# Low halves of split weights: adding transfers that read DRAM instead of the raw tile, sums of weights in place, six raw tiles

## The chip, the cores and the metric

The kernel runs on one core of one Trainium2 chip. The metric is device time in microseconds of the whole program, one launch. Times of several runs are given by their median. The page and the trace come from one further execution that was profiled.

## What is computed

Two layers of a trunk act on 640 tokens (128 context, 512 latent) of width 1024. Each layer has a half-step feed-forward, a mixer (windowed attention, pooling, short convolution) and a second half-step feed-forward; shift, scale and gate of each come from a modulation by `w_ada`. Cut to the part that matters here:

```
def ffn_sublayer(x, mod, k, g, w_in, w_out):
    h = modulated_norm(x, mod, k, g)
    gt, up = jnp.split(h @ w_in, 2, axis=-1)          # w_in: 1024 x 5632
    return x + 0.5 * mod[:, None, 3 * k + 2] * ((jax.nn.silu(gt) * up) @ w_out)   # w_out: 2816 x 1024

def trunk_layer(x, mod, ...):
    x = ffn_sublayer(x, mod, 0, norm_g[0], w_ffn_in[0], w_ffn_out[0])
    h = modulated_norm(x, mod, 1, norm_g[1])
    q, k, v, u_pool, u_conv, bg, cg = jnp.split(h @ w_in, IN_SPLITS, axis=-1)
    ...
    y = jnp.concatenate([attn, pool, conv], axis=-1) @ w_out
    x = x + mod[:, None, 5] * y
    return ffn_sublayer(x, mod, 2, norm_g[2], w_ffn_in[1], w_ffn_out[1]), k, v
```

All tensors are float32.

## The kernel before

Tokens lie along the free dimension, in two halves of 320 columns; channels lie on the 128 partitions. TensorE (PE) multiplies in float32r, a reduced form of float32. To keep float32's precision each operand is split in two: a high half `h` or `wh`, which is the operand rounded to float32r, and a low half `wl`, the rest. `mm3` (L351 to L354) then makes three products onto one accumulator: high by high (L352), high by low (L353), low by high (L354).

How a weight gets its halves is the matter here. A load on the SP queue brings 128 columns of a weight (or 256 of an output weight) into a raw tile of 128 x 1024 (`raw_tile`, L142; pool `raw`, five tiles). `split_w` (L164) has ScalarE (ACT) copy it to `wh` (L170), which rounds, and copy `-wh` to `wl` (L173). Then GpSimd (POOL) issues a DMA whose source is the raw tile and which adds to what stands in `wl` (L174): `wl = raw - wh`. The transfer runs on the 16 DMA engines that also run the loads. POOL's instruction at L174 is the issue alone. With another engine given, `split_w` subtracts there instead (L176). There are four `wh` and four `wl` tiles of full size and two small ones.

Weights are prefetched as far as tiles allow: the Tile scheduler orders each engine's instructions ahead of time and decides which tile takes over which buffer; a load on the SP queue waits until the buffer's last reader is done, and the loads behind it in the queue wait with it.

The feed-forward (`ffn`, L556) goes over 22 columns of 128 hidden channels (index `j`), each with an upper weight and a gate weight, and after every four or five of them multiplies the finished ones with rows of the output weight (`down`, L618; `update_x`, L518, adds the result to the residual on DVE). In the first feed-forward all columns are plain (`up`, L602). In the other three the first three are plain and 19 are fast (`fast_ups`, L690): seven products of half size instead of eight, by sums of weights. `fast_weights` (L640) loads the upper weight (halves a1, a2) and the gate weight (d1, d2), and DVE makes four sums (L646) into two tiles of a pool `sums` (`sum_tile`, L145; two tiles):

```
one = [a1+d1, d1+d2]      two = [d1+d2+a1, d1+d2+a1+a2]
products use: 1 = a1, 2 = a2, 4 = d2, 3 = two's second half, 6 = two's first, 5 = one's second, 7 = one's first
```

The upper weight and d2 get their low half from an adding transfer (512 KB and 256 KB), the two tiles of sums by subtraction on DVE (L176). On PE the order in a column is 1, then 3 and 4 of the column before, then 6, 2, 7, 5.

The modulation (`ada_steps`, L293) runs beside the feed-forwards: each step loads a 512 KB piece of `w_ada` into a raw tile. In the first feed-forward DVE sums over it into a tile of `sums` (L309, L311); later PE multiplies it directly (L275). `sums` also gives the tile that takes transposed probabilities in the attention (L1116). The last feed-forward carries no modulation.

The first column's weights are handled apart (`first_tiles`, L1218): `weights(0, nc.gpsimd)` splits the first pair by adding transfers, `weights(1, nc.vector)` the second by DVE.

## Time and profile before

| | us |
|---|---|
| median of three runs (2467.55 to 2479.46) | 2470.77 |
| profiled execution | 2474.73 |
| its span, first to last instruction | 2472.9 |
| PE busy | 2341.6 (95%) |
| PE weight loads busy | 2250.0 (91%) |
| DVE busy | 1324.6 (54%) |
| ACT busy | 1217.4 (49%) |
| POOL busy | 317.4 (13%) |

The stages lie at about these places of the span: first feed-forward to 490 us, mixer to 760, second feed-forward to 1240, then the second layer's feed-forward to 1700, mixer to 2010 and last feed-forward to the end. PE's weight loads run beside its products. DMA-issuing instructions of SP are not counted as busy; POOL's issue of a transfer is. "DMA share" is the mean busy share of the 16 DMA engines. Queue q1 is that of the loads issued by SP, q0 that of the transfers issued by POOL. A row of the timeline gives the start, the duration, the instruction, and in brackets how long its engine was idle before it and what ended that.

### The profile page before, as it was taken

To read this page: it belongs to the slowest core of one execution; us is meant where nothing else is said; L and a number is where in the kernel's file an instruction comes from. 1 tells how busy PE (TensorE), PEld (TensorE's weight loads), DVE (VectorE), ACT (ScalarE), POOL (GpSimd) and SP (SyncE) were. 2 spreads that over 40 slices of the span, in tenths; PEclk is the share of its full clock that TensorE was granted. 3 is DMA by queue.
4 is the path that set the end of the run, shared out by engine and by line. 5 is a ranking of instruction groups with operands and counts; after the bars stand their busy time and mean duration, and the time that the engine had idled before them with its cause. 6 is when DMAs were issued, how large, how long until landed. Compare 5 with 4: busy or idle time off the path is not lost.

```text
span 2472.9 us, 41585 instructions
## 1 busy us (share of the span) xinstructions
PE 2341.6 (95%) x16594; PEld 2250.0 (91%) x16594; DVE 1324.6 (54%) x2907; ACT 1217.4 (49%) x2080; POOL 317.4 (13%) x383
## 2 busy tenths in 40 slices
PE   7899999999999999989999999899999999999999
PEld 6899999989978998979999989899898789999999
DVE  4546565455868444345465353454557675445453
ACT  4433333445668444344565353445456675455461
POOL 1111111111100111110101111111111001111110
PEclk9999999999999999999999999999999999999999
DMA  8869798766524776775866767767665236666563
GB/s 279 208 160 247 184 258 196 206 144 137 134 56 116 191 161 180 166 196 141 204 144 157 159 146 170 176 151 174 153 129 130 59 81 132 155 130 162 131 156 101
DMA packets 388826, 393.13 MB, mean 159 GB/s; under 512 B 31032, under 2 KB 306840, under 8 KB 388632
## 3 DMA queue, kind: packets, MB, share of 16 engines
q1 hardware_dynamic: 340932, 244.88, 32.9%
q0 software_dynamic: 47520, 145.51, 32.7%
q8 instruction: 131, 2.15, 0.4%
q14 instruction: 63, 0.52, 0.1%
q10 hardware_dynamic: 180, 0.07, 0.0%
HBM read 242.04 MB, written 2.88 MB: 99 GB/s over the span
## 4 chain that ended last, share of the span: by engine, by line
PE 55%; issue 19%; DMA 16%; DVE 5%; ACT 3%; POOL 1%; POOLq 0%; ACTq 0%; SPq 0%; DVEq 0%
PE acc L352 16%; PE acc L353 16%; PE acc L354 16%; DMA wl<-raw 7%; DMA raw<-in_w_ffn_in 7%; POOL wl L174 1%; PE mis L275 1%; DMA raw<-in_w_ada 1%; DVE sums L646 1%; ACT wl L173 1%; PE acc L1060 1%; PE po L352 1%; PE mis L1111 1%; PE po L353 1%; PE po L354 1%
## 5 line engine op out<-in xcount | busy, mean ns | idle before, releaser
L352 PE MATMUL acc<-h,wh 128*128 128x320 f32 (+1 forms) x2808 | 886.4, 318 | 59.1 <-ACT part L671 24.5
L354 PE MATMUL acc<-h,wl 128*128 128x320 f32 (+1 forms) x2808 | 875.9, 313 | 15.5 <-DMA wl<-raw 15.4
L353 PE MATMUL acc<-h,wh 128*128 128x320 f32 (+1 forms) x2808 | 878.6, 314 | 0.6 <-DVE h L156 0.6
L170 ACT ACTIVATE wh<-raw 128x1024 fp32r<-128x1024 f32 (+2 forms) x332 | 305.5, 921 | 662.4 <-PE acc L353 438.1
L352 PEld LDWEIGHTS acc<-h,wh 128*128 128x128 f32 x2808 | 535.2, 191 | 81.3 <-ACT part L671 29.9
L354 PEld LDWEIGHTS acc<-h,wl 128*128 128x128 f32 x2808 | 535.8, 191 | 20.4 <-DMA wl<-raw 20.2
L174 POOL DMA_DIRECT2D wl<-raw x330 | 287.7, 872 | 2049.3 <-ACT wl L173 1425.5
L353 PEld LDWEIGHTS acc<-h,wh 128*128 128x128 f32 x2808 | 536.5, 191 | 2.9 <-POOL h L412 0.8
L352 PE MATMUL acc<-g,wh 128*128 128x320 f32 x1408 | 444.1, 315 | 33.5 <-DVE x L518 33.5
L353 PE MATMUL acc<-g,wh 128*128 128x320 f32 x1408 | 442.1, 314 | 0.0
L354 PE MATMUL acc<-g,wl 128*128 128x320 f32 x1408 | 441.3, 313 | 0.0
L518 DVE SCALAR_TENSOR_TENSOR x<-acc,gate,x 128x128 f32<-128x128 f32 (+2 forms) x480 | 195.3, 436 | 285.1 <-PE acc L354 283.8
L173 ACT ACTIVATE wl<-wh 128x1024 fp32r<-128x1024 f32 (+2 forms) x330 | 302.6, 917 | 4.7
L352 PEld LDWEIGHTS acc<-g,wh 128*128 128x128 f32 x1408 | 270.4, 192 | 37.9 <-DVE x L518 26.3
L353 PEld LDWEIGHTS acc<-g,wh 128*128 128x128 f32 x1408 | 270.6, 192 | 0.3
L354 PEld LDWEIGHTS acc<-g,wl 128*128 128x128 f32 x1408 | 270.2, 192 | 0.7 <-DMA wl<-raw 0.5
L170 ACT ACTIVATE wh<-sums 128x1024 fp32r<-128x1024 f32 x114 | 120.6, 1057 | 163.6 <-PE acc L353 145.9
L176 DVE TENSOR_TENSOR wl<-sums,wh 128x1024 fp32r<-128x1024 f32 x114 | 139.6, 1225 | 66.4 <-ACT wh L170 64.9
L646 DVE TENSOR_TENSOR sums<-raw 128x512 f32<-128x512 f32 x114 | 74.7, 688 | 167.5 <-DMA raw<-in_w_ffn_in 167.0
L311 DVE SCALAR_TENSOR_TENSOR sums<-raw,c,sums 128x512 f32<-128x512 f32 x196 | 134.7, 744 | 38.3 <-DMA raw<-in_w_ada 38.3
L671 ACT ACTIVATE part<-acc 128x320 f32<-128x320 f32 x171 | 72.9, 426 | 42.5 <-PE acc L354 42.4
L156 DVE TENSOR_TENSOR g<-part,g 128x320 fp32r<-128x320 f32 x114 | 56.0, 492 | 68.5 <-ACT g L155 67.6
(200 smaller groups left out, 2470.4 us busy)
## 6 DMA issues: line engine op xcount, KB each, us to landing
wl<-raw POOLq DMA_DIRECT2D x209, 512.0 KB, 5.2
raw<-in_w_ffn_in SPq DMA_DIRECT2D x176, 512.0 KB, 5.0
raw<-in_w_ada SPq DMA_DIRECT2D x128, 512.0 KB, 5.2
raw<-in_w_ffn_out SPq DMA_DIRECT2D x48, 512.0 KB, 4.2
raw<-in_w_ffn_out SPq DMA_DIRECT2D x64, 320.0 KB, 4.2
wl<-raw POOLq DMA_DIRECT2D x64, 320.0 KB, 4.5
wl<-raw POOLq DMA_DIRECT2D x57, 256.0 KB, 4.7
raw<-in_w_in SPq DMA_DIRECT2D x20, 512.0 KB, 5.7
```

Source lines behind the costliest of these rows:

```text
L156: nc.vector.tensor_tensor(lo, src, f32(h), op=ALU.subtract)
L170: nc.scalar.activation(h, raw, AF.Copy)
L173: nc.scalar.activation(lo, f32(h), AF.Copy, scale=-1.0)
L174: eng.dma_start(lo, raw, accum_op=ALU.add)
L176: eng.tensor_tensor(lo, raw, f32(h), op=ALU.subtract)
L311: nc.vector.scalar_tensor_tensor(part[:, j, :], r[:, k, :], c, part[:, j, :], op0=ALU.mult, op1=ALU.add)
L352: nc.tensor.matmul(out, wh, xh, start=start, stop=False, skip_group_check=onto)
L353: nc.tensor.matmul(out, wh, xl, start=False, stop=False, skip_group_check=onto)
L354: return nc.tensor.matmul(out, wl, xh, start=False, stop=stop, skip_group_check=onto)
L518: nc.vector.scalar_tensor_tensor(xT[t][:, s:e], ps[:, s - a : e - a], gates[l][n][:, t, j : j + 1], xT[t][:, s:e], op0=ALU.mult, op1=ALU.add,)
L646: add = lambda out, x, y: nc.vector.tensor_tensor(out, x, y, op=ALU.add)
L671: nc.scalar.activation(t, ps[:, :HALF], AF.Copy)
```

## The change

Four edits. The adding transfer reads the weight's columns from DRAM once more, by the same access pattern as the load, instead of the raw tile (`adding`; every load function now takes the function that starts the transfer). The sums of weights are made in place in the two raw tiles: afterwards the gate tile holds d1+d2 and a1+d1+d2, the upper tile a1+d1 and the sum of all four; both are then split by DVE as before. Pool `sums` goes; the raw pool has six tiles in place of five, and also gives the modulation's accumulator in the first feed-forward and the attention's tile. The first pair of weights is subtracted on POOL instead of by adding transfers. The scratch for descriptors that POOL writes grows from 1024 to 4096.

```
-    rawp = pool("raw", 5)
+    rawp = pool("raw", RAW)
-    sump = pool("sums", 2)
...
         raw = (raw or raw_tile())[:, : nk * width].rearrange("p (k c) -> p k c", k=nk)
-        loads(raw)
-        return raw, nk, width
+        loads(raw, nc.sync.dma_start)
+        return raw, nk, width, loads
+    def adding(dst, src):
+        nc.gpsimd.dma_start(dst, src, accum_op=ALU.add)
...
-    def split_w(raw, nk, width, eng=nc.gpsimd):
+    def split_w(raw, nk, width, loads=None, eng=None):
...
         nc.scalar.activation(h, raw, AF.Copy)
-        if eng is nc.gpsimd:
+        if eng is None:
             nc.scalar.activation(lo, f32(h), AF.Copy, scale=-1.0)
-            eng.dma_start(lo, raw, accum_op=ALU.add)
+            loads(lo, adding)
         else:
             eng.tensor_tensor(lo, raw, f32(h), op=ALU.subtract)
...
-            lambda raw: nc.sync.dma_start(raw, src[:, c0 : c0 + width].rearrange("(k p) c -> p k c", p=P)),
+            lambda dst, start: start(dst, src[:, c0 : c0 + width].rearrange("(k p) c -> p k c", p=P)),
...
-            part = sum_tile().rearrange("p (j c) -> p j c", j=2)
+            part = raw_tile().rearrange("p (j c) -> p j c", j=2)
...
-            one, two = view(sum_tile()), view(sum_tile())
-            ups = split_w(up, KD, P)
-            add(one[:, :nk, :], a1, d1)
-            add(one[:, nk:, :], d1, d2)
-            add(two[:, :nk, :], one[:, nk:, :], a1)
-            add(two[:, nk:, :], two[:, :nk, :], a2)
-            late = split_w(d2, nk, P)
-            twos = split_w(two, KD, P, nc.vector)
-            ones = split_w(one, KD, P, nc.vector)
+            ups = split_w(up, KD, P, up_loads)
+            late = split_w(d2, nk, P, lambda dst, start: start(
+                dst, w_in[D // 2 :, j * P : (j + 1) * P].rearrange("(k p) c -> p k c", p=P)))
+            add(a1, a1, d1)
+            add(d1, d1, d2)
+            add(d2, a1, d2)
+            add(a2, d2, a2)
+            gates = split_w(gate, KD, P, eng=nc.vector)
+            both = split_w(up, KD, P, eng=nc.vector)
...
-                    pts = sum_tile("pts")[:, :512]
+                    pts = raw_tile()[:, :512]
...
-            ws.extend(split_w(*raws[2 * j + s], eng=eng) for s in range(2))
+            ws.extend(split_w(*raws[2 * j + s][:3], eng=eng) for s in range(2))
...
-    nc = bacc.Bacc("TRN2", target_bir_lowering=False, num_devices=1, dynamic_dma_scratch_size=1024)
+    nc = bacc.Bacc("TRN2", target_bir_lowering=False, num_devices=1, dynamic_dma_scratch_size=4096)
```

Two places of the order are shown. First POOL's queue of adding transfers in the last fast columns of the second layer's first feed-forward; a row names destination, source, and partitions x elements (before) or partitions x pieces x elements (now). Before:

```order
L174 DMA wl<-raw 128x1024
L174 DMA wl<-raw 128x512
L174 DMA wl<-raw 128x1024
L174 DMA wl<-raw 128x512
L174 DMA wl<-raw 128x1024
L174 DMA wl<-raw 128x512
```

Now, the last columns and the output weights behind them:

```order
L162 DMA wl<-in_w_ffn_in 128x8x128
L162 DMA wl<-in_w_ffn_in 128x4x128
L162 DMA wl<-in_w_ffn_in 128x8x128
L162 DMA wl<-in_w_ffn_in 128x4x128
L162 DMA wl<-in_w_ffn_in 128x8x128
L162 DMA wl<-in_w_ffn_in 128x4x128
L162 DMA wl<-in_w_ffn_out 128x4x256 x8
```

The sequence of large and small transfers is as it was; the source is DRAM, and each partition's share is eight or four pieces of 128 elements.

Second the sums on DVE in the last feed-forward, one fast column and the start of the next (`part` are partial products, `g` the gated result). Before:

```order
L683 TENSOR_TENSOR part<-acc,part 128x320
L156 TENSOR_TENSOR g<-part,g 128x320
L675 TENSOR_TENSOR part<-acc,part 128x320
L687 TENSOR_TENSOR part<-part 128x320
L156 TENSOR_TENSOR g<-part,g 128x320
L675 TENSOR_TENSOR part<-po,part 128x320
L176 TENSOR_TENSOR wl<-sums,wh 128x1024
L646 TENSOR_TENSOR sums<-raw 128x512 x2
L176 TENSOR_TENSOR wl<-sums,wh 128x1024
L675 TENSOR_TENSOR part<-acc,part 128x320
L646 TENSOR_TENSOR sums<-sums,raw 128x512 x2
```

Now:

```order
L683 TENSOR_TENSOR part<-acc,part 128x320
L646 TENSOR_TENSOR raw<-raw 128x512
L153 TENSOR_TENSOR g<-part,g 128x320
L675 TENSOR_TENSOR part<-acc,part 128x320
L646 TENSOR_TENSOR raw<-raw 128x512 x2
L687 TENSOR_TENSOR part<-part 128x320
L646 TENSOR_TENSOR raw<-raw 128x512
L153 TENSOR_TENSOR g<-part,g 128x320
L675 TENSOR_TENSOR part<-po,part 128x320
L176 TENSOR_TENSOR wl<-raw,wh 128x1024 x2
L675 TENSOR_TENSOR part<-acc,part 128x320
```

The four sums stood around the two subtractions and belonged to the column after; now they stand ahead of the two subtractions that read them, between the column's other work.

## Rows read from the trace of the kernel before

**Rows 1.** The page: busy us (share of the span) xinstructions, by engine

```profile
PE 2341.6 (95%) x16594; PEld 2250.0 (91%) x16594; DVE 1324.6 (54%) x2907; ACT 1217.4 (49%) x2080; POOL 317.4 (13%) x383
```

**Rows 2.** Waits of PE: who waited for whom, us in total, times, longest

```profile
PE acc L352 <- DVE x L518: 41.5, 13, 6.9
PE acc L352 <- ACT part L671: 24.5, 17, 3.3
PE acc L354 <- DMA wl<-raw: 15.4, 13, 4.7
```

**Rows 3.** Windows: stretch, its us, busy (x) of five engines, clock, DMA share, GB/s

```profile
100.00:490.00 390.00, 379.05 (x2677) 372.03 (x2676) 207.73 (x453) 142.34 (x210) 50.38 (x58) 0.98 0.84 211
...
760.00:1240.00 480.00, 447.32 (x3456) 432.04 (x3455) 232.16 (x448) 233.52 (x374) 60.84 (x70) 0.97 0.72 176
1240.00:1700.00 460.00, 429.26 (x3144) 415.92 (x3143) 233.07 (x443) 224.40 (x366) 56.91 (x66) 0.98 0.66 157
2010.00:2410.00 400.00, 385.08 (x2561) 382.92 (x2560) 215.42 (x383) 214.82 (x346) 55.95 (x65) 0.98 0.62 141
```

**Rows 4.** Timeline of SP's queue, then of DVE, second feed-forward

```profile
1078.20 14.34 SPq L181 DMA_DIRECT2D raw<-in_w_ffn_out  x4
...
1104.68 1.29 DVE L646 TENSOR_TENSOR sums<-raw 128x512 f32<-128x512 f32 x2 [7.79 <-DMA raw<-in_w_ffn_in]
```

**Rows 5.** DMA queues, 2020.4 to 2023.8 us: one 256 KB add alone

```profile
q0 software_dynamic: 144, 0.26, 44.1%
```

**Rows 6.** DMA queues, 1374.3 to 1378.1 us: one 320 KB add alone

```profile
q0 software_dynamic: 144, 0.33, 47.5%
```

**Rows 7.** DMA queues, 467.2 to 471.8 us: one 512 KB add alone

```profile
q0 software_dynamic: 144, 0.52, 59.7%
```

**Rows 8.** DMA queues (packets, MB, share) and issues, 100 to 490 us

```profile
q1 hardware_dynamic: 64267, 55.17, 45.3%
q0 software_dynamic: 8208, 26.74, 37.9%
...
wl<-raw POOLq DMA_DIRECT2D x42, 512.0 KB, 5.9
...
wl<-raw POOLq DMA_DIRECT2D x16, 320.0 KB, 4.4
```

**Rows 9.** DMA queues, 326 to 398 us

```profile
q1 hardware_dynamic: 13164, 11.56, 51.6%
q0 software_dynamic: 1363, 4.96, 37.5%
```

**Rows 10.** Timeline of POOL, then of ACT, two fast columns, last feed-forward

```profile
2151.32 0.88 POOL L174 DMA_DIRECT2D wl<-raw  x1 [11.67 <-ACT wl L173]
...
2163.68 0.86 POOL L174 DMA_DIRECT2D wl<-raw  x1 [10.08 <-DVE part L675]
...
2160.90 1.06 ACT L170 ACTIVATE wh<-raw 128x1024 fp32r<-128x1024 f32 x1 [0.30 <-PE acc L353]
...
2162.23 1.04 ACT L173 ACTIVATE wl<-wh 128x1024 fp32r<-128x1024 f32 x1
```

**Rows 11.** DMA issues, 2163.5 to 2168.5 us: KB each, us to landing

```profile
wl<-raw POOLq DMA_DIRECT2D x1, 512.0 KB, 4.6
```

**Rows 12.** Timeline of PE at the next column's first product

```profile
2169.98 0.31 PE L354 MATMUL acc<-h,wl 128*128 128x320 f32 x1
```

**Rows 13.** POOL by line: count, busy us, mean ns, idle before and what ended it

```profile
L174 POOL DMA_DIRECT2D wl<-raw x330 | 287.7, 872 | 2049.3 <-ACT wl L173 1425.5 <-DVE part L675 173.9 <-ACT part L671 96.2
L930 POOL TENSOR_TENSOR rope<-qw,turn 128x512 f32<-128x512 f32 x8 | 10.4, 1296 | 33.0 <-DVE qw L918 33.0
```

**Rows 14.** Timeline of POOL, then of PE, first column

```profile
21.34 1.01 POOL L174 DMA_DIRECT2D wl<-raw  x1 [19.66 <-ACT rr L389]
...
29.60 0.64 PE L354 MATMUL acc<-h,wl 128*128 128x320 f32 x1 [4.66 <-DMA wl<-raw]
```

**Rows 15.** The page's DMA queues: packets, MB, share of 16 engines

```profile
q0 software_dynamic: 47520, 145.51, 32.7%
```

More of the change, by code (lines that the diff above doesn't have):

```diff
@@ L49 @@
 TMPS = 9
+RAW = 6
 KEYS = ((0, 3, 3), (0, 4, 1), (1, 5, 1), (2, 5, 0))
@@ L143, in raw_tile @@
         return rawp.tile([P, 1024], F32, tag="raw", name="raw")
-    def sum_tile(name="sums"):
-        return sump.tile([P, 1024], F32, tag="sums", name=name)
     def load_ada(l, ci, q, tile):
@@ L642, in fast_weights @@
             nk = KD // 2
-            up, *_ = load_raw(w_in, DFF + j * P)
+            up, *_, up_loads = load_raw(w_in, DFF + j * P)
             gate, *_ = load_raw(w_in, j * P)
@@ L646, in fast_weights @@
             add = lambda out, x, y: nc.vector.tensor_tensor(out, x, y, op=ALU.add)
-            view = lambda t: t.rearrange("p (k c) -> p k c", k=KD)
-            one, two = view(sum_tile()), view(sum_tile())
-            ups = split_w(up, KD, P)
-            add(one[:, :nk, :], a1, d1)
-            add(one[:, nk:, :], d1, d2)
-            add(two[:, :nk, :], one[:, nk:, :], a1)
-            add(two[:, nk:, :], two[:, :nk, :], a2)
-            late = split_w(d2, nk, P)
-            twos = split_w(two, KD, P, nc.vector)
-            ones = split_w(one, KD, P, nc.vector)
+            ups = split_w(up, KD, P, up_loads)
[7 more added lines that the diff above has]
+            both = split_w(up, KD, P, eng=nc.vector)
             first = lambda w: (w[0][:, :nk, :], w[1][:, :nk, :])
             second = lambda w: (w[0][:, nk:, :], w[1][:, nk:, :])
-            return {1: first(ups), 2: second(ups), 3: second(twos), 4: late, 5: second(ones), 6: first(twos), 7: first(ones)}
+            return {1: first(ups), 2: second(ups), 3: second(both), 4: late, 5: first(gates), 6: second(gates), 7: first(both)}
         def fast_product(ps, w, x, start):
@@ L990, in mixer, with loads @@
         for a in range(4):
-            def loads(raw):
+            def loads(dst, start, a=a):
                 for g in range(2):
                     c = g * 256 + a * HD
-                    nc.sync.dma_start(
-                        raw[:, :, g * HD : (g + 1) * HD],
+                    start(
+                        dst[:, :, g * HD : (g + 1) * HD],
                         w_in[:, c : c + HD].rearrange("(k p) c -> p k c", p=P),
@@ L1152, in second_product, with loads @@
             for m2 in range(4):
-                def loads(raw):
+                def loads(dst, start, m2=m2):
                     for g in range(2):
-                        nc.sync.dma_start(
-                            raw[g * HD : (g + 1) * HD, :, :],
+                        start(
+                            dst[g * HD : (g + 1) * HD, :, :],
                             w_out[g * 256 : (g + 1) * 256, m2 * 256 : (m2 + 1) * 256].rearrange(
```

## The prediction

> **What bounds the kernel now.** I read the page first: the matrix engine (PE) is busy 95% of the span [rows 1]. So the floor is PE's own work, and a change here can only move the few per cent in which PE waits. The waits of PE by releaser come next [rows 2]: 41.5 us in 13 waits for VectorE's (DVE's) residual update at L518, 24.5 us for ScalarE's (ACT's) copy at L671, 15.4 us for an adding transfer into `wl`. Of the idle 131 us (2472.9 less 2341.6) these three are 81, and all three lead back to weights that come late. Then the windows by stage [rows 3]: PE is busy 379 of 390 us in the first feed-forward, 447 of 480 and 429 of 460 in the two fast ones that also carry adaLN weights, 385 of 400 in the last, at a granted clock of 0.97 or 0.98 of the full one. The DMA engines' share in the same rows is 0.84, 0.72, 0.66 and 0.62: the transfers are the second load of this kernel, and in the first stage a close second.
>
> One of those waits shows where the first two come from [rows 4]. The SP queue needed 14.34 us to issue four loads of `w_ffn_out`, each held until a raw tile was free; only after that, at 1092.5, could the next two `w_ffn_in` loads start; DVE, which works in order, stood 7.79 us before the sums of that tile, and the residual updates behind those sums let PE wait. A raw tile is held there until its adding transfer has landed.
>
> **The change, part by part.** Durations are of the one profiled execution: 2474.73 us, span 2472.9; the median of the three timed runs is 2470.77, 4 us less. Half a per cent, about 12 us, is what a measurement of this kernel can tell from no change.
>
> *What an adding transfer costs a DMA engine.* Before, its source is a raw tile in SBUF: 128 pieces of 4, 2.5 or 2 KB, 8 for each of 16 engines. Now it is the weight matrix in DRAM, whose rows give pieces of 512 bytes (`w_ffn_in`, `w_in`, the five-tile chunks of `w_ffn_out`), 1 KB (256 columns wide) or 256 bytes (queries). The trace has no such add, so I go by three adds that ran alone [rows 5, 6, 7]. Share times window is busy time of each engine: 44.1% of 3.4 = 1.50 us for 256 KB, 47.5% of 3.8 = 1.81 us for 320 KB, 59.7% of 4.6 = 2.75 us for 512 KB, always 8 data packets. From 2 KB to 4 KB a packet goes from 0.188 to 0.343 us: 0.076 us for each KB, so 0.032 us are there whatever the size; the middle row fits (0.226 against 0.227). That line gives 0.071 us for 512 bytes. A 512 KB add is then 64 packets, 4.5 us instead of 2.75; a 320 KB one 40 packets, 2.8 instead of 1.8; the 256 KB one of the fast stage 2.3 instead of 1.5; 1 KB pieces 3.5 instead of 2.75; a query tile 128 packets of 0.051 us, 6.6 instead of 2.75. The lower bound is that the bytes alone count: 2.75 as before. I take the line, because three rows lie on it. The Trainium skill, page DMA: Bandwidth & Descriptors, section Specifications, gives 512 bytes as the smallest transfer at line rate. By it the add would stay at 2.75 us and the sum below would turn into the first rival; the fixed 0.032 us in [rows 5 to 7] speak against it for adding packets.
>
> *First feed-forward (100 to 490 us).* It has 42 adds of 512 KB and 16 of 320 KB [rows 8]: 42 x 2.75 + 16 x 1.81 = 144 us, against 37.9% of 390 = 148 shown. Now 42 x 4.5 + 16 x 2.8 = 234. The loads take 45.3%, 177 us. Together 411 us for a stage that took 390: here the DMA engines become the bound. At a full share that is 21 us more. The fullest long stretch of the trace, 326 to 398 us, reaches 51.6 + 37.5 = 89% [rows 9]; at that share it is 72 us more. I take **+45**, the middle.
>
> *The fast columns (57: 19 in each of three stages).* Each issues one 512 KB and one 256 KB add. In the last stage a column takes 12.36 us (adds of 512 KB at 2151.32 and 2163.68 [rows 10]). The upper weights' copy at 2160.90 waits for PE's third product, which frees the buffer; the negated copy is at 2162.23, the add issued at 2163.68, landing 4.6 us later [rows 10, 11] at 2168.28. PE first reads those low weights at 2169.98 [rows 12], 1.7 us later: that slack covers it today. The change moves none of this ahead; it lengthens it. The packets add 4.5 - 2.75 = 1.8 us, just the slack. To this comes the issue. POOL takes 0.872 us for an add, the mean over all 330 [rows 13], always for 128 pieces. For 1024 pieces the lower bound is the same 0.87 us (all of it fixed), the upper eight times as much, 7.0 us (all of it by the piece). No row lies between; I take 2.5 us, the geometric middle, for ends a factor of eight apart. So the landing moves 1.8 + 1.6 = 3.4 us, 1.7 beyond the slack: 57 x 1.7, about **+95**. With the upper bound it is 57 x 6.2 = 353, with the lower next to nothing. The same page's section Anatomy of one DMA says that many descriptors can be emitted before their cost shows. By it the issue stays near 0.9 us and this term is gone, which is the second rival.
>
> *Raw tiles.* A tile of the plain and output weights is now free after ACT's copy, some 6 us sooner (negated copy 1.04, wait for the issue, landing 4.6, [rows 10, 11]), and there are six. In the fast columns a pair is held longer, until DVE's second split. What this can win is bounded by [rows 2]: the 81 us of weight waits above, below by nothing. I take **-20**, near the lower end, since loads that start sooner now share fuller DMA engines. The adaLN accumulator of the first feed-forward also takes one of the six.
>
> *Sums in place.* Same number of DVE adds and splits. In the changed order they stand behind ACT's two reads of the same halves and ahead of the splits; the first needed product is a column away. Nothing.
>
> *First column.* Its two adds become POOL subtractions. POOL takes 1.296 us for 512 columns [rows 13], so at most 2.6 for 1024. The first add was issued at 21.34 and PE waited 4.66 us for it until 29.60 [rows 14]; nearly all of that wait goes: **-4**.
>
> *Queries.* Eight tiles at 3.9 us more DMA work: 31 at most, nothing where the four low-weight buffers hide it. I take the quarter, since those buffers reach some tiles ahead: **+8.**
>
> Sum: 45 + 95 - 20 - 4 + 8 = +124 us on 2474.7, 2599; on the median **2595 us**.
>
> **The rivals.** *Raw tiles decide (faster).* If an add packet of 512 bytes costs no more than its bytes (below about 0.045 us) and POOL issues in under 1.5 us, adds land as now and stages are not full. What is left is the earlier release of raw tiles at the start of the output products, as in [rows 4]. For it: that wait is plainly one for tiles. Against it: [rows 5 to 7]. Price: half of the 81 us, 2475 - 40 - 4, on the median 2427. Chance 0.22.
>
> *Only the first stage is full.* Packets cost what the line says, but descriptors are cheap to write: +45 + 8 - 20 - 4, on the median 2500. For it: 1.8 us and 1.7 us of slack nearly meet. Chance 0.18.
>
> *Gains and costs meet.* Packets near 0.055 us: within 0.5%, 2471. Chance 0.10.
>
> *POOL becomes the bound.* At 7 us for 1024 pieces a plain column with two adds needs 14 us of POOL, and every fast column is 6.2 us late: 2475 + 353 + 45, about 2870. Against it: nothing in the trace, but a fixed part of the 0.87 us is likely. Chance 0.08.
>
> **How the numbers follow.** The forecast, slower through late adds and a full first stage, has 0.42; its own range is 2510 to 2740, where 2740 is an issue of 4.4 us (57 x 3.5 = 200), a first stage at 89% (72) and no gain from raw tiles. For 8 in 10 I add the second rival, the middle one and a part of the first: 2440 to 2740. Faster 0.22, same 0.10, slower 0.42 + 0.18 + 0.08 = 0.68.
>
> **What would show it.** POOL's mean for an add well above 0.872 us; q0's share up from 32.7% to near 48% [rows 15] with some 260 thousand packets; in the first stage a DMA share above 0.93; waits of PE for `wl` up from 15.4 us to 60 or more, in the fast columns; SP's long issues before the output weights shorter. I am wrong if q0's share stays below 36%, if landing stays near 5 us, or if PE's waits for `wl` stay where they are.

## The result and the profile after

| | before | after |
|---|---|---|
| median of four runs each, us | 2469.16 | 2635.91 |
| span of the profiled execution, us | 2472.9 | 2634.0 |
| PE busy, us | 2341.6 | 2396.5 |
| mean granted clock of PE | 0.977 | 0.948 |

The change is slower: the ratio of after to before is 1.0668, interval 1.0624 to 1.0712. The forecast was 2595, slower with 0.68; direction and range held. Where the time went is another matter. One execution of the last experiment below, 3185.88 us at a mean granted clock of 0.653, is a slow one and is left out of that experiment's median.

The page's busy times, to be read against [rows 1]:

```profile
PE 2396.5 (91%) x16594; PEld 2282.3 (87%) x16594; DVE 1333.6 (51%) x2907; ACT 1222.4 (46%) x2078; POOL 531.7 (20%) x399
```

PE executes the same 16594 products, and its busy time is 55 us longer, at the lower clock; the other 106 us of the loss are idle time. POOL's busy time went from 317 to 532 us.

The page's DMA queues, which answer to [rows 15], and POOL's lines of the adding transfers, which answer to [rows 13]:

```profile
q0 software_dynamic: 263040, 144.46, 42.9%
q1 hardware_dynamic: 340932, 244.88, 31.2%
...
L162 POOL DMA_DIRECT2D wl<-in_w_ffn_in x172 | 255.7, 1535 | 1054.3 <-ACT wl L173 619.0
...
L162 POOL DMA_DIRECT2D wl<-in_w_ffn_out x112 | 163.7, 1481 | 478.0 <-ACT wl L173 416.4
```

Nearly the same bytes (145.51 MB before) now go in 263 thousand packets instead of 47.5 thousand, and an issue takes 1.5 us on the mean in place of 0.872. The windows with the bounds of [rows 3]:

```profile
100.00:490.00 390.00, 367.96 (x2564) 359.76 (x2563) 196.49 (x425) 135.63 (x198) 82.49 (x54) 0.97 0.97 201
760.00:1240.00 480.00, 439.85 (x3246) 408.54 (x3245) 238.99 (x528) 241.72 (x427) 92.61 (x66) 0.96 0.75 156
1240.00:1700.00 460.00, 437.26 (x3229) 424.36 (x3228) 229.80 (x447) 232.62 (x375) 99.44 (x69) 0.98 0.84 171
```

The first feed-forward runs at a DMA share of 0.97 (before 0.84). From 760 us on the same bounds cover another piece of work, since the stages have moved. So I cut both traces at events of the program instead: a stage of feed-forward or mixer begins with the last product of its norm on PE (L375), and the attention part with the first product of scores (L1060). Projections are what lies between. (Cut so, the first feed-forward of before ends at 545.8 us; the forecast reckoned with its stretch from 100 to 490.) Stage times in us, from PE's timeline (FF is feed-forward):

| | first FF | proj. 1 | att. 1 | second FF | third FF | proj. 2 | att. 2 | last FF |
|---|---|---|---|---|---|---|---|---|
| before | 545.8 | 113.4 | 113.1 | 511.5 | 496.7 | 112.6 | 116.7 | 463.1 |
| after | 569.3 | 146.7 | 167.4 | 492.6 | 479.8 | 147.3 | 167.5 | 463.4 |
| difference | +23.5 | +33.3 | +54.3 | -18.9 | -16.9 | +34.7 | +50.8 | +0.3 |

The differences add up to 161.1, which is the difference of the spans. **The two mixers, a fifth of the program, lose 173 us; the three fast feed-forwards, where the forecast put its largest loss, win 35.5.** The waits of PE say the same in another way (answering to [rows 2]):

```profile
PE acc L354 <- DMA wl<-in_w_ffn_in: 44.6, 21, 5.5
PE acc L354 <- DMA wl<-in_w_in: 32.0, 10, 5.8
PE acc L354 <- DMA wl<-in_w_ffn_out: 29.6, 10, 4.8
PE mis L1111 <- DVE pr L1091: 27.3, 8, 5.0
PE mis L916 <- ACT tmp L909: 23.6, 2, 11.9
PE mis L265 <- DVE arow L264: 16.1, 5, 5.0
```

L1111 and L916 lie in the mixers, `w_in` is the projections' weight, L265 is the modulation. The waits for L518 and L671 that led [rows 2] are no longer among the first.

What happens in the projections is seen on POOL (timeline: start, duration, instruction, idle before it and what ended that; "issue" is idle time for which the profile shows no cause):

```profile
645.50 1.57 POOL L162 DMA_DIRECT2D wl<-in_w_in  x1 [3.48 <-PE acc L354]
650.57 1.56 POOL L162 DMA_DIRECT2D wl<-in_w_in  x1 [3.50 <-issue]
655.68 1.57 POOL L162 DMA_DIRECT2D wl<-in_w_in  x1 [3.55 <-issue]
...
660.84 1.56 POOL L162 DMA_DIRECT2D wl<-in_w_in  x1 [3.27 <-issue]
665.85 1.57 POOL L162 DMA_DIRECT2D wl<-in_w_in  x1 [3.45 <-issue]
666.76 1.95 POOL L930 TENSOR_TENSOR rope<-kv,turn 128x512 f32<-128x512 f32 x1
```

The queries' transfers start every 5.1 us and never overlap (the one of 645.50 lands 4.8 us after its issue), and the rotation of the keys (L930), which needs nothing of them, stands behind them in POOL's queue. The same is seen in plain columns of the first feed-forward, with a period of 6.6 us:

```profile
132.03 1.56 POOL L162 DMA_DIRECT2D wl<-in_w_ffn_in  x1 [5.40 <-issue]
138.61 1.57 POOL L162 DMA_DIRECT2D wl<-in_w_ffn_in  x1 [5.02 <-issue]
145.35 1.56 POOL L162 DMA_DIRECT2D wl<-in_w_ffn_in  x1 [5.17 <-issue]
```

Over the whole program POOL's idle time without a cause is 253 us:

```profile
POOL wl L162 <- issue: 253.3, 46, 9.6
```

In the attention it is SP's queue. First its timeline, then its waits (whom a load waited for, us in total, times, longest):

```profile
712.18 58.53 SPq L181 DMA_DIRECT2D raw<-in_w_out  x3
799.40 23.97 SPq L1156 DMA_DIRECT2D raw<-in_w_out  x8
```

```profile
SPq L181 <- PE po L1100: 120.0, 11, 26.8
SPq L1156 <- PE po L1100: 94.4, 6, 29.9
```

Three loads of output weights took 58.5 us to issue; they waited for L1100, the products that read the transposed probabilities, which since the change lie in raw tiles.

**Theory A** before the experiments: (1) in the projections, POOL's scratch of 4096 has no room for a second transfer of 1024 pieces, so that each waits for the one before; (2) in the attention, the probabilities' tiles block the loads of output weights; (3) in the first feed-forward, transfers from DRAM or the accumulator's raw tile or both. Rivals: the many packets make the output weights late whatever the tiles are (B); POOL waits for something else, or the DMA engines are full in any case (D); the tiles cause the projections' loss too (C).

### The profile page after: what moved, and what is told of

Its sections match the earlier page's. It is cut to its first block, busy times and chain, and to the rows that moved or that the text cites. A ratio compares the mean times of both kernels' runs of the same rounds, so it can differ in the third digit from the quotient of the medians.

```text
span 2634.0 us, 41552 instructions
## 1 busy us (share of the span) xinstructions
PE 2396.5 (91%) x16594; PEld 2282.3 (87%) x16594; DVE 1333.6 (51%) x2907; ACT 1222.4 (46%) x2078; POOL 531.7 (20%) x399
## 3 DMA queue, kind: packets, MB, share of 16 engines
q0 software_dynamic: 263040, 144.46, 42.9%
## 4 chain that ended last, share of the span: by engine, by line
PE 55%; issue 21%; DMA 11%; DVE 4%; POOL 4%; ACT 3%; POOLq 0%; ACTq 0%; SPq 0%; DVEq 0%
PE acc L354 16%; PE acc L352 16%; PE acc L353 16%; POOL wl L162 3%; DMA wl<-in_w_ffn_in 3%; DMA wl<-in_w_ffn_out 3%; DMA raw<-in_w_ada 2%; PE mis L275 1%; DVE raw L311 1%; DMA wl<-in_w_in 1%; PE po L353 1%; PE po L354 1%; PE po L352 1%; ACT wh L171 1%; DMA wl<-in_w_out 1%
## 5 line engine op out<-in xcount | busy, mean ns | idle before, releaser
L354 PE MATMUL acc<-h,wl 128*128 128x320 f32 (+1 forms) x2808 | 885.7, 316 | 76.9 <-DMA wl<-in_w_ffn_in 44.6
L171 ACT ACTIVATE wh<-raw 128x1024 fp32r<-128x1024 f32 (+2 forms) x446 | 425.9, 957 | 830.1 <-PE acc L353 740.4
L162 POOL DMA_DIRECT2D wl<-in_w_ffn_in x172 | 255.7, 1535 | 1054.3 <-ACT wl L173 619.0
L518 DVE SCALAR_TENSOR_TENSOR x<-acc,gate,x 128x128 f32<-128x128 f32 (+2 forms) x480 | 195.8, 436 | 321.6 <-PE acc L354 319.3
L162 POOL DMA_DIRECT2D wl<-in_w_ffn_out x112 | 163.7, 1481 | 478.0 <-ACT wl L173 416.4
L176 DVE TENSOR_TENSOR wl<-raw,wh 128x1024 fp32r<-128x1024 f32 x116 | 142.1, 1225 | 119.4 <-ACT wh L171 118.7
L646 DVE TENSOR_TENSOR raw<-raw 128x512 f32<-128x512 f32 x228 | 157.0, 689 | 41.6 <-ACT wh L171 20.9
L311 DVE SCALAR_TENSOR_TENSOR raw<-raw,c 128x512 f32<-128x512 f32 x196 | 136.4, 747 | 66.2 <-DMA raw<-in_w_ada 66.2
L162 POOL DMA_DIRECT2D wl<-in_w_in x36 | 56.3, 1565 | 229.9 <-ACT wl L173 82.7
L352 PE MATMUL acc<-mix,wh 128*128 128x320 f32 x256 | 89.1, 348 | 12.6 <-ACT wh L171 10.5
```

The lines of the kernel that those rows point to most:

```text
L162: nc.gpsimd.dma_start(dst, src, accum_op=ALU.add)
L171: nc.scalar.activation(h, raw, AF.Copy)
L176: eng.tensor_tensor(lo, raw, f32(h), op=ALU.subtract)
L311: nc.vector.scalar_tensor_tensor(part[:, j, :], r[:, k, :], c, part[:, j, :], op0=ALU.mult, op1=ALU.add)
L352: nc.tensor.matmul(out, wh, xh, start=start, stop=False, skip_group_check=onto)
L354: return nc.tensor.matmul(out, wl, xh, start=False, stop=stop, skip_group_check=onto)
```

## The experiments

Stage times of all runs, in us, cut as above (F1 to F4 the feed-forwards, P and A projections and attention). Each row is one profiled execution. The timed runs of one kernel spread over 4 to 24 us, so a difference of a few us in one stage says little; the profiled execution of e7_fast_dram lies 11 us below the median of its six.

| | F1 | P1 | A1 | F2 | F3 | P2 | A2 | F4 | span |
|---|---|---|---|---|---|---|---|---|---|
| before | 545.8 | 113.4 | 113.1 | 511.5 | 496.7 | 112.6 | 116.7 | 463.1 | 2472.9 |
| after | 569.3 | 146.7 | 167.4 | 492.6 | 479.8 | 147.3 | 167.5 | 463.4 | 2634.0 |
| e1_pts_own | 569.1 | 149.6 | 121.7 | 505.7 | 480.6 | 151.0 | 121.2 | 465.1 | 2564.0 |
| e3_add_from_raw | 568.7 | 114.6 | 156.0 | 501.0 | 475.0 | 114.5 | 151.9 | 474.6 | 2556.3 |
| e5_scratch_5888 | 575.8 | 121.1 | 164.5 | 491.3 | 473.7 | 120.1 | 164.0 | 464.7 | 2575.2 |
| e6_halves | 582.1 | 151.2 | 121.9 | 506.3 | 474.8 | 150.1 | 122.0 | 467.6 | 2576.0 |
| e7_fast_dram | 570.8 | 112.2 | 113.7 | 488.4 | 462.3 | 112.5 | 116.7 | 460.0 | 2436.6 |
| e9_raw_source_six | 554.5 | 113.0 | 113.4 | 501.4 | 476.5 | 112.6 | 113.1 | 478.1 | 2462.6 |
| e10_slots_fast_dram | 564.0 | 115.1 | 119.0 | 476.0 | 462.2 | 113.0 | 115.5 | 455.0 | 2419.8 |
| e11_slots_dram | 567.9 | 149.7 | 124.7 | 492.8 | 479.7 | 148.2 | 125.6 | 459.3 | 2547.9 |
| e13_slots_dram_5888 | 554.5 | 120.9 | 119.5 | 489.3 | 477.2 | 121.2 | 119.6 | 459.1 | 2461.3 |
| e14_first_pair_adds | 566.5 | 115.1 | 117.9 | 474.2 | 462.1 | 112.7 | 115.7 | 458.3 | 2422.5 |
| e15_in_place_alone | 537.3 | 112.6 | 113.4 | 517.1 | 485.7 | 112.7 | 116.8 | 476.0 | 2471.6 |
| e17_sums_fast_dram | 545.8 | 112.2 | 114.8 | 490.0 | 461.6 | 114.9 | 115.8 | 463.9 | 2419.0 |

### One suspect at a time: the probabilities' tile, the source, the scratch

```
+    ptsp = pool("pts", 2)
-RAW = 6
+RAW = 5
...
-                    pts = raw_tile()[:, :512]
+                    pts = ptsp.tile([P, 512], F32, tag="pts", name="pts")
```

> The changed kernel, but the attention's transposed probabilities get two tiles of 128 x 512 of a pool of their own, and the raw pool has five tiles instead of six (the memory allows no more). Theory A: the attention stretch of each mixer (716.0 to 861.5 us in the first) became 49 us longer because the probabilities take raw tiles from the output weights' loads; then it goes back from 145 us to 96 to 105, in both mixers, the projection stretch (147 us) stays within 5 us, and the time is 2540 to 2580 us, the missing sixth raw tile costing 0 to 35 us in the feed-forwards. Rival B: the adding transfers' many descriptors make the output weights late; then the attention stays at 140 us or more and the time at 2630 us or above.

2566.44 us, ratio 1.0368 (1.0336 to 1.0400). The attention fell from 167.4 and 167.5 to 121.7 and 121.2 us, the projections stayed; rival B falls. (The expectations count the attention up to the first half's product of the next norm, 861.5 us in after; the table cuts at the second half's, 883.4. By the first count e1_pts_own has 96.0 and 95.5 us in the two mixers, where 96 to 105 was expected.) SP's queue in the first attention no longer stands before an output weight; the last four of these loads (L1156, here L1157) go out before it begins, at 718.7 us:

```profile
704.72 9.36 SPq L1157 DMA_DIRECT2D raw<-in_w_out  x4
```

The shared tile is shown to be the attention's cause for 46 of its 51 to 54 us.

```
-            loads(lo, adding)
+            adding(lo, raw)
```

> The changed kernel, but the adding transfers read the raw tile again, as in the kernel before; in-place sums, six raw tiles and shared pool stay. Theory A: the source in DRAM costs the first feed-forward 24 us and each mixer's projections 33 us; both go back (first feed-forward's end 569 to about 545, projections 147 to 114 to 120 us), while the attention stays at 140 to 148 us; the sums in place must now wait for the transfer that reads the raw tile, which costs the three fast feed-forwards between 0 and 60 us; the time is 2530 to 2600 us. Rival C: the tiles (in place, shared pool) cause the projections' loss too; then they stay at 140 us or more and the time is 2610 us or above.

2558.16 us, ratio 1.0326 (1.0298 to 1.0353). The projections are back at 114.6 and 114.5, so their loss is the source's and not the tiles': rival C falls. The attention stays long, at 156.0 and 151.9 (138 and 135 by the expectation's count, a little less than its 140 to 148). The first feed-forward did not come back: 568.7. That part of theory A fell. PE now waits for the modulation; 23.6 of the first row's 33.5 us are in that stage:

```profile
PE mis L265 <- DVE arow L264: 33.5, 11, 10.9
PE acc L354 <- DMA wl<-raw: 28.5, 25, 2.0
```

```
-dynamic_dma_scratch_size=4096
+dynamic_dma_scratch_size=5888
```

> The changed kernel, but with a scratch for POOL's descriptors of 5888 in place of 4096. Theory A: with 4096 a transfer of 1024 pieces finds no room until the one before it is done, which is POOL's unexplained idle time of 5.0 us before its issues (periods of 6.6 us in the first feed-forward); with room for two the idle time before those issues falls below 2 us, the projections shrink from 147 to 115 to 130 us each, the first feed-forward ends 10 to 24 us earlier, attention stays at 145 us; the time is 2560 to 2600 us. Rival D: POOL waits for something else, or the DMA engines are full in any case; then the periods stay at 6.6 us, the projections at 140 us or more, and the time at 2620 to 2645 us.

2578.83 us, ratio 1.0415 (1.0387 to 1.0442): one number wins 57 us. The projections take 121.1 and 120.1 instead of 147; POOL's unexplained idle time is 46.8 us instead of 253.3, and transfers of the projections start in pairs:

```profile
POOL wl L162 <- issue: 46.8, 14, 5.3
```

```profile
644.11 3.15 POOL L162 DMA_DIRECT2D wl<-in_w_in  x2 [0.29 <-ACT tmp L896]
649.42 1.31 POOL L930 TENSOR_TENSOR rope<-kv,turn 128x512 f32<-128x512 f32 x1 [2.16 <-issue]
652.57 3.17 POOL L162 DMA_DIRECT2D wl<-in_w_in  x2 [1.84 <-ACT wl L173]
```

So the wait was one for scratch, and it makes 26 to 27 of the projections' 33 to 35 us; rival D falls. Against the expectation, the idle time before such an issue is still 3.3 us on the mean, not below 2, and the first feed-forward did not gain (575.8).

### The first feed-forward, and what the source is worth where

```
+    halfp = pool("halves", 2)
...
-            part = raw_tile().rearrange("p (j c) -> p j c", j=2)
+            part = [half_tile(), half_tile()]
...
-                    pts = raw_tile()[:, :512]
+                    pts = half_tile()
```

> The changed kernel, but the modulation's accumulator in the first feed-forward and the attention's probabilities take tiles of 128 x 512 of a pool of their own (two tiles), raw tiles five. All adding transfers read DRAM. Theory A: the 23 us that the first feed-forward lost are the accumulator's, which holds one raw tile of six while the loads of the modulation wait for one; then it ends at 545 to 552 us instead of 569, the attention (from the first scores to the last norm) takes 117 to 125 us instead of 167, the projections stay at 147 us, and the time is 2535 to 2565 us. Rival E: the first feed-forward loses by the transfers' demand on the DMA engines; then it ends at 562 us or later and the time is 2560 to 2590 us.

2578.06 us, ratio 1.0428 (1.0392 to 1.0464). The attention behaves as expected (121.9), the first feed-forward does not: 582.1, the longest of all. Stage and time lie where rival E has them. It is not shown by that, since the two half tiles make one accumulator only, where the kernel before had two to alternate.

```
+            if dram:
+                loads(lo, adding)
+            else:
+                adding(lo, raw)
...
-            ups = split_w(up, KD, P, up_loads)
+            ups = split_w(up, KD, P, up_loads, dram=True)
```

> As the run with tiles of their own for accumulator and probabilities, but only the two adding transfers of a fast column read DRAM; those of the plain columns, the output weights and the mixer read the raw tile. Theory A: the projections take 114 us again, the attention 113 to 117, the first feed-forward ends at 545 to 548 us, the second and third feed-forward keep what the sums in place gave them (490 to 508 and 472 to 485 us); the time is 2435 to 2465 us, below the kernel before. Rival F: the gain of the fast feed-forwards hung on the output weights' transfers too or on the sixth raw tile; then the second feed-forward is at 512 us or more and the time is 2470 to 2500 us.

(Likewise for `late`.) 2449.15 us, ratio 0.9891 (0.9864 to 0.9918): **1.1% faster than the kernel before, clear of the interval.** Projections and attention are back, the second and third feed-forward win 23 and 34 us. The first still ends at 570.8, though all its transfers read the raw tile: 11 us earlier than with DRAM as the source, 25 later than before.

```
-RAW = 5
+RAW = 6
...
-            loads(lo, adding)
+            adding(lo, raw)
...
-dynamic_dma_scratch_size=4096
+dynamic_dma_scratch_size=1024
```

> As the run with tiles of their own for accumulator and probabilities, but with six raw tiles, all adding transfers from the raw tile and the scratch of 1024 of the kernel before. What is left of the change is the sums in place, the sixth raw tile and the first pair on POOL. Theory A: first feed-forward ends at 545 us or earlier, projections 114, attention 113 to 117; second, third and last feed-forward as in the run with adds from the raw tile (501, 475 and 475 us) within 8 us; the time is 2440 to 2470 us. Rival G: without DRAM as the source the sums in place, which wait for the transfer out of the raw tile, cost as much as the sixth tile gives; then the three fast feed-forwards together take 1471 us or more and the time is 2465 to 2490 us.

(The edits stand against e6_halves.) 2464.99 us, ratio 0.9951 (0.9933 to 0.9969). The sums in place now wait for the transfer that reads the tile they overwrite (waits of DVE):

```profile
DVE raw L650 <- DMA wl<-raw: 128.8, 68, 6.7
```

Still the fast feed-forwards take 1456.0 together, against 1471.3 before, so rival G falls by its stages (its time, 2465 us or more, is missed by a hair); the first ends at 554.5, not at 545.

```
-            part = raw_tile().rearrange("p (j c) -> p j c", j=2)
+            part = slot(name="part", shape=(2, 512))
...
-                    pts = raw_tile()[:, :512]
+                    pts = slot(name="pts", shape=(512,))
```

> The changed kernel, six raw tiles, but the modulation's accumulator and the attention's probabilities take tiles of the pool slots, and only the two adding transfers of a fast column read DRAM. Theory A, amended: the first feed-forward loses by two things, either of which is enough: transfers from DRAM, and an accumulator that has no second tile beside the loads' own (25 us in the run with two half tiles, five raw tiles and adds from the raw tile there); with neither it ends at 540 to 550 us. Projections 112 to 114, attention 113 to 120 us, second feed-forward at 495 or less and third at 470 or less; the time is 2395 to 2440 us, the fastest so far. Rival H: the first feed-forward's loss is that of the first pair on POOL, or of an order that shifted; then it ends at 560 us or later again and the time is 2425 to 2460 us.

(With the `dram` edit of e7_fast_dram.) 2415.65 us, ratio 0.9784 (0.9758 to 0.9811), the lowest median. The fast feed-forwards take 1393.2 us, 62.8 less than in e9_raw_source_six: that is what reading DRAM is worth in the fast columns. (The scratch differs too, 4096 against 1024. e3_add_from_raw, with 4096 and the raw source, has 1450.6, so 57 us are left if the scratch is held.) The sums on DVE no longer wait for an adding transfer, only for the ACT copy and the loads:

```profile
DVE raw L649 <- ACT wh L171: 18.3, 46, 0.7
DVE raw L649 <- DMA raw<-in_w_ffn_in: 14.5, 9, 3.0
```

and SP's loads (L181 before, L184 here) wait for adding transfers for 843 us where it was 1353 us before (the splits on DVE now hold them for another 371):

```profile
SPq L184 <- DMA wl<-raw: 843.0, 134, 37.3
```

```profile
SPq L181 <- DMA wl<-raw: 1353.4, 222, 37.0
```

The second feed-forward now is 466 of 476 us PE, where it was 478 of 512 before. The first, at 564.0, lies where rival H has it and theory A has not; the time is below rival H's 2425.

```
-            if dram:
-                loads(lo, adding)
-            else:
-                adding(lo, raw)
+            loads(lo, adding)
```

> As the run with slots for accumulator and probabilities, but all adding transfers read DRAM, as in the change. What is left between the two is the source of the transfers outside of the fast columns. Theory A: first feed-forward 15 to 36 us later than there (DMA share above 0.9), projections 147 instead of 113 us, attention 5 to 10 us longer, fast feed-forwards within 15 us; the time is 85 to 130 us above that run's. Rival I: the queries and the first feed-forward lose only in company of the shared tiles; then the difference is below 60 us.

(Against e10_slots_fast_dram: `split_w` as in the change.) 2548.30 us, ratio 1.0325 (1.0296 to 1.0355), 133 above e10_slots_fast_dram, a little more than theory A's 130 and far from rival I's 60. The parts differ from the expectation: projections +35 each and attention +6 and +10 as expected, the first feed-forward only +3.9, but second and third +17 each. In these two stages (842.3 to 1814.8 us) PE waits 19.7 us for the output weights' low halves and 17.4 for those of `w_ffn_in`; in e10_slots_fast_dram (798.1 to 1736.3 us) it waits 16.3 us for all adding transfers together.

```profile
PE acc L354 <- DMA wl<-in_w_ffn_out: 19.7, 6, 4.2
PE acc L354 <- DMA wl<-in_w_ffn_in: 17.4, 12, 5.2
```

```
-dynamic_dma_scratch_size=4096
+dynamic_dma_scratch_size=5888
```

> As the run with slots and all adding transfers from DRAM, with a scratch of 5888 for POOL's descriptors. Theory A: the projections go from 147 to 121 us each, as they did when this alone was changed, the first feed-forward stays within 10 us, the time is 40 to 60 us below that run's. Rival D: with the tiles out of the way the scratch no longer matters; then the projections differ by less than 10 us.

(Against e11_slots_dram.) 2463.65 us, ratio 0.9979 (0.9963 to 0.9995): 85 us below, well above the expected 40 to 60. 56 are the projections' (121 each), the first feed-forward gives 13, where 10 at most was expected. With two tiles moved and one number raised, the change as it was written no longer loses: within half a per cent, hence no difference by the bound given ahead.

### What is left in the first feed-forward

```
-        weights(0, nc.gpsimd)
+        weights(0, None)
```

> The fastest kernel so far (slots for accumulator and probabilities, six raw tiles, only fast columns add from DRAM), with the first pair of weights split by adding transfers as in the kernel before, not on POOL. Theory A: the first pair on POOL gains 3 us at the first column and costs nothing later; the first feed-forward ends 3 to 5 us later or within 8 us of 564, and the time is 2410 to 2425 us. Rival H: the subtraction on POOL shifts the order behind it, and that is the 18 us that the first feed-forward still loses; then it ends at 545 to 550 us and the time is 2395 to 2405 us.

(Against e10_slots_fast_dram.) 2422.97 us, ratio 0.9782 (0.9740 to 0.9823). The first feed-forward ends at 566.5: rival H's first form, the pair on POOL, falls. With the pair on POOL the stage is 2.5 us shorter, which is the way theory A has it but no more than two single executions can differ; the ratios are the same.

```
-RAW = 6
+RAW = 5
...
+    sump = pool("sums", 2)
...
-            loads(lo, adding)
+            adding(lo, raw)
...
-            part = raw_tile().rearrange("p (j c) -> p j c", j=2)
+            part = sum_tile().rearrange("p (j c) -> p j c", j=2)
...
-                    pts = raw_tile()[:, :512]
+                    pts = sum_tile("pts")[:, :512]
...
-dynamic_dma_scratch_size=4096
+dynamic_dma_scratch_size=1024
```

> The kernel before with two edits alone: sums in place, and the first pair on POOL. Five raw tiles, two tiles of sums (for accumulator and probabilities), all adding transfers from the raw tile, scratch 1024. Theory A: projections 113 and attention 113 to 117 us as before; the first feed-forward ends at 540 to 550 us, since its accumulator has two tiles and its loads five again; in the fast feed-forwards the sums in place wait for the transfer that reads the raw tile, and with no sixth raw tile to make up for it they take 1471 us or more together (before: 1471); the time is 2465 to 2500 us. Rival H: the first feed-forward ends at 555 us or later through the first pair's place alone.

2475.64 us, ratio 1.0005 (0.9982 to 1.0028). The first feed-forward ends at 537.3: with two accumulators of their own it is at its best. The fast ones take 1478.8, 7.5 more than before. DVE waits for the transfers out of the raw tile:

```profile
DVE raw L650 <- DMA wl<-raw: 141.9, 71, 7.2
```

Sums in place without a source in DRAM give nothing, and e9_raw_source_six against this run puts the sixth raw tile at 22.8 us in the fast stages.

```
-TMPS = 9
+TMPS = 8
...
-            ups = split_w(up, KD, P, up_loads)
+            ups = split_w(up, KD, P, up_loads, dram=True)
...
-dynamic_dma_scratch_size=1024
+dynamic_dma_scratch_size=3136
```

> Five raw tiles and the two tiles of sums of the kernel before (for accumulator and probabilities), sums in place, the first pair on POOL, and only the two adding transfers of a fast column from DRAM; to make room, one of nine small working tiles is gone and the scratch is 3136. Theory A: the first feed-forward ends at 537 to 545 us (as with these pools before), projections 113, attention 113 to 117, and the fast feed-forwards take what they took with five raw tiles and this source (488, 462, 460 us); the time is 2395 to 2415 us, 0 to 20 us below the run with slots. Rival J: the missing working tile or the smaller scratch costs the fast columns what the first feed-forward gains; then the time is 2415 to 2445 us.

(Against e15_in_place_alone, with the `dram` edit of e7_fast_dram in full.) 2419.21 us, ratio 0.9771 (0.9740 to 0.9803), no different from e10_slots_fast_dram. The first feed-forward ends at 545.8, but the fast stages take 1415.5 instead of 1393.2 with five raw tiles. The two places of the memory trade evenly. The time lies in rival J's range, 4 us above theory A's; but e7_fast_dram, with five raw tiles, nine working tiles and a scratch of 4096, has 1411.0 in the fast stages, so what rival J names costs them 5 us at most.

## Why the prediction was right, and where it was wrong

The sum said +124 on a profiled execution of 2474.7; +161 was measured (2635.83). **The direction was right for a part of the reasons; that the size came near is luck, two errors that met:** the fast feed-forwards were put at +95 less 20 and came at -35.5, the mixers were put at +8 and came at +173. Point by point:

**What an adding transfer costs a DMA engine: right.** One 512 KB transfer from 512-byte pieces stands alone at 2174.8 to 2181.5 us of after (6.7 us), one 256 KB transfer at 2186.8 to 2193.0 (6.2 us), one 512 KB transfer from 1 KB pieces at 743.5 to 750.0 (6.5 us), and one of a query, 256 KB from 256-byte pieces, at 650.5 to 655.5 (5.0 us):

```profile
q0 software_dynamic: 1040, 0.52, 63.7%
...
q0 software_dynamic: 528, 0.26, 34.5%
...
q0 software_dynamic: 528, 0.52, 54.9%
...
q0 software_dynamic: 1040, 0.26, 59.5%
```

The first three are 4.3, 2.1 and 3.6 us for each engine; the line through [rows 5 to 7] said 4.5, 2.3 and 3.5. The bytes alone would have been 2.75, 1.5 and 2.75. The Trainium skill, page DMA: Bandwidth & Descriptors, section Specifications, gives 512 bytes as enough for line rate; for adding transfers these rows disagree. Source and size of the pieces changed together here; but the query's transfer makes 3.0 us of each engine in 64 data packets, and the three sizes from DRAM, 0.047, 0.067 and 0.112 us a packet, lie on a line with some 0.025 us fixed (an estimate from these rows), so a fixed part is there with DRAM as the only source too.

**First feed-forward, +45: the stage lost 23.5, and full DMA engines do not explain it.** They did become full: 0.97 in the window, q0 at 51.9% of 390 us, 202 us in place of 148. But e13_slots_dram_5888 has the same share there, with q0 at 52.1%, and ends the stage at 554.5, 8.7 us later than before; and e3_add_from_raw, which reads the raw tile, ends it as late as the change does.

```profile
100.00:490.00 390.00, 370.54 (x2598) 363.24 (x2598) 212.60 (x453) 138.30 (x199) 84.92 (x56) 0.97 0.97 205
```

With the accumulator out of the raw pool, reading DRAM cost 3.9 us (e10_slots_fast_dram against e11_slots_dram), and 11 with half tiles. The step took every microsecond that the engines lack as one of PE's.

What costs the stage its 23.5 us is shown in part. With the accumulator in a raw tile PE waits 16 to 24 us there for the modulation (L265, in four runs), and not at all before. Moving the accumulator to slots, which is all that differs for this stage in three pairs, gains 1.4 us in the change itself (against e11_slots_dram), 4.7 with the raw source (e3_add_from_raw against e10_slots_fast_dram) and 21.3 with the scratch of 5888 (e5_scratch_5888 against e13_slots_dram_5888); the larger scratch alone gains nothing, and both together 14.8. So with transfers from DRAM the accumulator's tile and the scratch each hold the stage up as long as the other is left. What is left even without either (554.5, and 564.0 with the raw source) stays open. The two experiments with the two old tiles of sums end the stage at 537 and 546 us, all others at 554 to 582; but they also have five raw tiles and a scratch of 1024 and 3136. Why slots don't serve as well as these tiles isn't settled; in e10_slots_fast_dram PE waits only 7.8 us for the accumulator itself, and what else shifted in the order there was not tried apart.

**Fast columns, +95: wrong, in sign too.** The issue was mis-sized, 1.56 us for 1024 pieces instead of 2.5; with it the same step would have given 57 x 0.8, about +45. Even that lateness hardly shows: in the three fast feed-forwards PE waits 20.4 us, in 12 waits, for adding transfers of `w_ffn_in`, the plain columns' among them. The step that failed is "The change moves none of this ahead". It does: the raw tiles no longer wait for the adding transfer, nor do the sums that overwrite them. Reading DRAM in the fast columns won 57 to 63 us over the raw source with the same tiles in these stages. In the change itself the stages won 35.5 us, since the output weights' and plain columns' transfers gave back 38.6 (e11_slots_dram less e10_slots_fast_dram, second to last feed-forward).

**Raw tiles, -20: too small.** The fast stages with tiles and source as in e10_slots_fast_dram win 78 us over before, about the whole 81 of [rows 2] that the text gave as the bound above: sums in place cost 7.5, the sixth raw tile gives 22.8 and the source in DRAM 62.8. The rival "raw tiles decide" had that mechanism and the right place; it lost because the change also took tiles away, for the probabilities and the accumulator, and because the scratch held up the transfers outside of the fast columns: with other tiles for the two users, 85 us hang on the scratch alone (e11_slots_dram against e13_slots_dram_5888). Its condition on the price of a packet did not hold.

**Queries, +8 in a range of 0 to 31: the two projections lost 68.** The step counted DMA work, 3.9 us a tile, and had that about right (two transfers of 3.0 us a tile by the last row above, where the line said 6.6 in all). What decided was scratch: each transfer had to wait for the one before, whatever the engines had free, and that makes 26 to 27 us in each (e5_scratch_5888). Their share in the projections was 0.58 in after, and 0.67 before. The change's own line on the scratch of 4096 was in the diff, and the prediction left it uncosted.

**The attention: no term at all, +105, of which the tile makes 92 (e1_pts_own).** The prediction noted that the accumulator takes one of six raw tiles, and passed over the probabilities, which take others in turn at L1116, in the middle of the output weights' loads.

**First column, -4: right in kind, a little large.** The wait of 4.66 us at 29.60 [rows 14] is gone; POOL's subtraction took 2.402 us, as bounded, and PE waits 3.92 us for `h` shortly before instead. Its first product with a low weight begins 2.6 us sooner, at 27.04 (27.24 in e10_slots_fast_dram, 29.51 in e14_first_pair_adds):

```profile
22.28 0.41 PE L352 MATMUL acc<-h,wh 128*128 128x320 f32 x1 [1.83 <-ACT h L411]
26.61 0.63 PE L353 MATMUL acc<-h,wh 128*128 128x320 f32 x1 [3.92 <-DVE h L412]
27.04 0.47 PE L354 MATMUL acc<-h,wl 128*128 128x320 f32 x1
```

**What would show it:** POOL's mean above 0.872, q0's share up (42.9%, not 48), 263 thousand packets, a share of 0.97 in the first stage came true. "Waits of PE for `wl` of 60 or more, in the fast columns" was right in size and wrong in place: of the changed kernel's 106 us in three rows, 32 are the projections' and 30 the output weights', and of the 45 for `w_ffn_in` 20 at most can be the fast columns'.

The clock adds to the waits in the mixers. In the attention of before and of after (`659.00:772.00` and `716.00:883.00` us: length, then busy us of PE and the others, granted clock, DMA share, GB/s):

```profile
659.00:772.00 113.00, 110.44 (x726) 91.31 (x725) 78.44 (x273) 77.48 (x190) 6.96 (x8) 1.00 0.32 73
```

```profile
716.00:883.00 167.00, 130.48 (x723) 102.79 (x723) 81.42 (x274) 83.15 (x193) 16.74 (x14) 0.87 0.38 79
```

PE needs 20 us more for the same products, at a mean granted clock of 0.87 instead of 1.00, which is to say that it spent a part of the stretch at 1.2 GHz and before all of it at 2.4: of the 54 us that this stage lost, 34 are waiting and 20 are slower work around the waits.

## What to carry to other kernels

When a pool is dissolved into another, list every tile that it served, not the one that the edit is about: here one short-lived user, the probabilities, cost 92 us, and the other, the accumulator, 21 in the first feed-forward where the scratch was no limit (1 where it was), against a gain of 78 that was to be had. When a transfer's pieces become smaller, look at three prices apart: engine time for each packet, the issue, and the room for descriptors, which turned a queue into one transfer at a time and cost 57 us until one number was raised. And a change that gains in one stage and loses in others is worth taking apart by stage: restricted to the columns whose tiles it frees, with the two users given tiles elsewhere, it is 2.2% faster than before (1.9 to 2.4).

## What the runs showed of the hardware

Writing eight times as many pieces made POOL's issue 1.56 us from 0.872, far from eight times. The Trainium skill, page DMA: Bandwidth & Descriptors, section Anatomy of one DMA, says that many descriptors can be written before their cost shows; these rows agree in kind, with 0.69 us for 896 more pieces.

A transfer of 1024 pieces in a scratch of 4096 let no second one start: periods of 6.6 and 5.1 us, which the profile shows as idle time of POOL without a cause; at 5888 they came in pairs. Everything behind such an issue on POOL's queue waits too: the rotation of the keys was done 99 us after the projections began (668.7 less 569.3), before the change 67 us after (613.0 less 545.8).
